# Two expert stores moved from the SyncE queue into the GpSimd ring, behind the last weight load

## The chip, the cores and the metric

The kernel runs on one core of a Trainium2 chip. The metric is the time on the device in microseconds, the median over several executions. Three executions of the kernel before gave 185.68, 185.75 and 185.85 us, so the median is 185.75 us. The execution that was profiled spans 183.8 us from its first to its last instruction; all positions in time below are microseconds from the start of that span.

## The reference

Eight experts, each with its own tokens and its own two weight matrices, computed independently:

```python
n_experts, capacity, hidden, expert_hidden = 8, 256, 512, 2048
# x [8,256,512]  w1 [8,512,2048]  w2 [8,2048,512]  b1 [8,2048]  b2 [8,512], all float32
h = np.matmul(x, w1) + b1[:, np.newaxis, :]
h = np.maximum(h, 0)
return (np.matmul(h, w2) + b2[:, np.newaxis, :]).astype(np.float32)
```

Each weight matrix of each expert is 4 MB in float32 in the device's memory (HBM), and is used once. Together with x the kernel has to read 71.4 MB, and it has to write 4.2 MB of output, 512 KB for each expert.

## The kernel before, in words

Every load of weights is a DMA issued from GpSimd that casts float32 to float16 on its way into the on-chip memory (SBUF), so a matrix of 4 MB arrives as 2 MB. Such a matrix is one DMA, with two exceptions: `w2` of expert 6 comes in two halves of 1 MB (`load_w2`, L78), and `w2` of the last expert, 7, comes in eight pieces (`load_w2_piece`, L87). A piece is named here by its place: p0 holds rows 0 to 3 of the 16 blocks of the inner dimension, p1 rows 4 to 6, p2 rows 7 to 9, p3 rows 10 and 11, all of the full width of 512 columns. Then the columns are cut at 320: p4 and p5 hold rows 12, 13 and 14, 15 of the first 320 columns, p6 and p7 the same rows of the last 192 columns.

For expert e, `first_product` (L107) multiplies x with w1 on TensorE (PE) in 16 blocks, and ScalarE (ACT) adds b1 and applies the maximum with zero. `second_product` (L150) multiplies the result with w2 and adds b2 in PSUM, and `store` (L133) copies the two halves of the result out of PSUM, one on VectorE (DVE, L137) and one on ACT (L138), into a tile of `out_pool`, which has three buffers. The main loop (L240) runs eleven steps: in step s it does the first product of expert s and the second product of expert s - 3. So the second products of experts 5, 6 and 7 fall in steps 8, 9 and 10, in which there is no first product left, and the work on PE in these steps follows directly on the arrival of w2.

The order of the DMAs on GpSimd is written out by hand. The list `ring` (L220 to L238) holds entries of a step, a function and its arguments; at the start of step s all entries at the head of the list that are due are issued (L241 to L243). GpSimd issues them in this order, and each waits for the DMA that came eight places earlier on GpSimd to land, since the DMAs of GpSimd share eight semaphores.

How an expert's output is stored depends on its number:

- Experts 0 to 4 (`e <= RING`, L143): the store is put aside in `pending` and issued from GpSimd by `flush` (L129), at its place in the ring. The store of expert 3 lies ahead of p0, that of expert 4 between p0 and p1.
- Experts 5 and 6 (L148): the store is issued from the SyncE queue (SP) as soon as the copies are done.
- Expert 7: its first 320 columns are stored from SP at L148 in one DMA of 320 KB. Its last 192 columns are stored in two DMAs of 96 KB, from SP (L141) and from ACT (L142).

The profile calls the queue of GpSimd q0, that of SP q1 and that of ACT q10. All three are served by the same 16 DMA engines of the core.

Of the kernel before, what the change touches and what calls it, by code (L numbers as in the profile page):

```python
# [11 lines left out]
def kernel(  # L12
# [17 lines left out]
    nJ = M // P  # L30
    HL = 320
    LAG = 3
    RING = 4
    PARTS = {}
    nXF32 = 2

# [96 lines left out]
    def store(e, po, c0, c1, split):  # L133
        w = c1 - c0
        pool = out_pool if w == H else singles
        out_sb = pool.tile([P, nTB, w], fp32, tag=f"out{c0}_{w}", name=f"out{w}")
        nc.vector.tensor_copy(out=out_sb[:, 0, :], in_=po[0])  # L137
        nc.scalar.copy(out=out_sb[:, 1, :], in_=po[1])  # L138
        dst = out[e].rearrange("(p tb) h -> p tb h", tb=nTB)[:, :, c0:c1]
        if split and c1 == H:  # L140
            nc.sync.dma_start(out=dst[:, 0, :], in_=out_sb[:, 0, :])  # L141
            nc.scalar.dma_start(out=dst[:, 1, :], in_=out_sb[:, 1, :])  # L142
        elif e <= RING:  # L143
            pending[e] = (dst, out_sb)
        else:
            step = P // PARTS.get(e, 1)
            for lo in range(0, P, step):
                nc.sync.dma_start(out=dst[lo : lo + step], in_=out_sb[lo : lo + step])  # L148

    def second_product(e):  # L150
# [18 lines left out]
        for lo, hi, p0, p1, t in w2_sb[e]:  # L169
            mine = [b for b in blocks if p0 <= b[0] and b[1] <= p1]  # L170
            for tb in range(nTB):
                for j in range(lo, hi):
                    for c0, c1, _, _ in mine:
                        ordered(nc.tensor.matmul(  # L174
                            out=acc[c0, tb],
                            lhsT=hT[e][:, j, tb * P : (tb + 1) * P],
                            rhs=t[:, j - lo, c0 - p0 : c1 - p0],
                            start=False,
                            stop=(j == nJ - 1),
                        ))  # L180
            if hi == nJ:
                for c0, c1, _, _ in mine:
                    store(e, [acc[c0, tb] for tb in range(nTB)], c0, c1, e == E - 1)
# [36 lines left out]
    ring = []  # L220
# [9 lines left out]
    e = E - LAG - 1  # L230
    for piece in (
        (0, 4, 0, H), (4, 7, 0, H), (7, 10, 0, H), (10, 12, 0, H),
        (12, 14, 0, HL), (14, 16, 0, HL), (12, 14, HL, H), (14, 16, HL, H),
    ):
        ring.append((0, load_w2_piece, (E - 1,) + piece))
        if e <= RING:
            ring.append((e + LAG + 1, flush, (e,)))
            e += 1  # L238

    for s in range(E + LAG):  # L240
        while ring and ring[0][0] <= s:  # L241
# [37 lines left out]
```

## Time and profile before

| what | value |
|---|---|
| median of three executions | 185.75 us |
| span of the profiled execution | 183.8 us |
| HBM read / written | 71.39 MB / 4.19 MB |
| PE busy | 137.3 us (75%) |
| ACT busy | 62.7 us (34%) |
| DVE busy | 13.3 us (7%) |
| GpSimd busy | 21.0 us (11%) |
| packets on q0, share of 16 DMA engines' span | 95.3% (37.76 MB) |
| packets on q1 | 3.1% (2.00 MB) |
| packets on q10 | 1.1% (0.69 MB) |
| store of expert 5: issued, landed after | 160.9 us, 8.2 us |
| store of expert 6: issued, landed after | 168.5 us, 7.1 us |
| last load, p7: issued, landed after | 169.34 us, 10.0 us |
| last stores of expert 7: issued, landed after | 180.16 and 180.23 us, 2.7 and 2.4 us |

The profile counts a load by the bytes that arrive, so a load in float16 counts half of what is read from HBM, and a store counts in full. The share of the DMA engines in a stretch can pass 1.00[...]. An idle time is put down to what ended it. "Landed" is the moment when the semaphore of a DMA had its full count, counted from the start of the issuing instruction. [...]

### The profile page before, as it was taken

The numbers are of one execution on the slowest core, as the hardware profiler recorded it, in microseconds if no ns is written. First come the engines' busy times: TensorE is split into PE (matmuls) and PEld (weight loads), VectorE is DVE, ScalarE is ACT, GpSimd is POOL, SyncE is SP. The second block draws the span as 40 slices with busy tenths as digits, with TensorE's granted clock in tenths as the row PEclk, the third lists the DMA queues.
The fourth block names the chain that finished last, engine by engine and source line by source line (L and its number), as shares of the span: only waits on it lengthen the run. The fifth ranks groups of instructions, "written<-read, shape, count | busy, mean of one in ns | idle before, by whom it ended". The sixth has DMA issues, their size and how long they took to land.

```text
span 183.8 us, 2205 instructions
## 1 busy us (share of the span) xinstructions
PE 137.3 (75%) x946; PEld 98.2 (53%) x946; DVE 13.3 (7%) x22; ACT 62.7 (34%) x138; POOL 21.0 (11%) x44
## 2 busy tenths in 40 slices
PE   0555969487471999569991999529999996998581
PEld 0544959387461846556491846427469543344360
DVE  0320101001000101010100100001010010101000
ACT  0022869578260422715081513605129310101001
POOL 7100030301200011011011002000022004113000
PEclk9999999999876699979999699965999999999998
DMA  5999999899999999999999999899999999999993
GB/s 185 283 207 198 228 228 210 184 233 230 228 203 196 228 228 217 194 216 228 228 210 200 217 228 228 191 266 225 207 200 270 240 209 260 214 275 310 261 151 116
DMA packets 7017, 40.58 MB, mean 221 GB/s; under 512 B 1216, under 2 KB 2256, under 8 KB 4960
## 3 DMA queue, kind: packets, MB, share of 16 engines
q0 software_dynamic: 5584, 37.76, 95.3%
q1 hardware_dynamic: 976, 2.00, 3.1%
q10 hardware_dynamic: 448, 0.69, 1.1%
q8 instruction: 7, 0.11, 0.2%
q14 instruction: 2, 0.02, 0.0%
HBM read 71.39 MB, written 4.19 MB: 411 GB/s over the span
## 4 chain that ended last, share of the span: by engine, by line
DMA 70%; PE 14%; issue 9%; another core or an unknown queue 3%; POOL 2%; ACT 0%; POOLq 0%
DMA x<-in_x_dram 24%; DMA w2sb<-in_w_dram 21%; DMA w1sb<-in_w_dram 13%; DMA w<-in_w_dram 12%; PE ph L112 6%; PE acc L174 6%; PE psx L99 1%; POOL w2sb L84 1%; POOL w1sb L74 1%; POOL out_dram L131 0%; PE acc L162 0%; POOL b_sb L190 0%; POOL ident masks.py:199 0%; POOL ident masks.py:197 0%
## 5 line engine op out<-in xcount | busy, mean ns | idle before, releaser
L112 PE MATMUL ph<-xT,w1sb 128*128 128x256 f16 x512 | 68.2, 299 | 11.6 <-DMA w1sb<-in_w_dram 11.6
L119 ACT ACTIVATE hT<-ph,b1T 128x256 f16<-128x256 f32 x128 | 57.0, 474 | 44.2 <-PE ph L112 44.2
L112 PEld LDWEIGHTS <-w1sb 128*128 128x128 f16 x512 | 61.5, 149 | 17.7 <-DMA w1sb<-in_w_dram 12.6
L174 PE MATMUL acc<-w2sb,hT 128*128 128x512 f16 x224 | 49.5, 379 | 1.6 <-DMA w2sb<-in_w_dram 1.6
L174 PEld LDWEIGHTS <-hT 128*128 128x128 f16 x288 | 27.2, 98 | 35.0 <-issue 9.0
L138 ACT COPY out<-acc 128x512 f32<-128x512 f32 (+2 forms) x9 | 4.9, 543 | 62.0 <-PE acc L174 62.0
L99 PE MATMUL psx<-ident,x 128*128 128x128 f16 x64 | 6.7, 266 | 18.8 <-DMA x<-in_x_dram 18.1
L99 PEld LDWEIGHTS <-x 128*128 128x128 f16 x64 | 5.2, 127 | 19.8 <-DMA x<-in_x_dram 19.0
L105 DVE COPY xT<-psx 128x1024 f16<-128x1024 f16 x8 | 5.5, 692 | 82.2 <-PE psx L99 82.2
L74 POOL DMA_DIRECT2D w1sb<-in_w_dram x8 | 4.4, 554 | 59.6 <-PE ph L112 58.8
L137 DVE COPY out<-acc 128x512 f32<-128x512 f32 (+2 forms) x9 | 5.7, 632 | 75.5 <-PE acc L174 75.5
L174 PE MATMUL acc<-w,hT 128*128 128x320 f16 (+1 forms) x64 | 7.7, 272 | 3.8 <-DMA w<-in_w_dram 3.7
L84 POOL DMA_DIRECT2D w2sb<-in_w_dram x8 | 4.3, 537 | 49.4 <-PE acc L174 49.4
L205 PE MATMUL pb<-ident,b_rows 16*64 16x16 f32 x64 | 3.7, 265 | 6.8 <-DMA b_rows<-in_b_dram 6.8
L205 PEld LDWEIGHTS pb<-ident,b_rows 16*64 16x64 f32 x64 | 3.6, 198 | 6.8 <-issue 6.8
L90 POOL DMA_DIRECT2D w<-in_w_dram x8 | 5.0, 623 | 13.0 <-DMA w2sb<-in_w_dram 8.8
L119 ACT ACT_TABLE_LOAD x1 | 1.3, 1283 | 11.2 <-DVE b1T L213 11.2
L131 POOL DMA_DIRECT2D out_dram<-out x5 | 2.7, 540 | 19.5 <-ACT out L138 13.1
L162 PE MATMUL acc<-b_sb,ones 1*128 1x512 f16 (+2 forms) x18 | 4.8, 355 | 0.0
L68 POOL DMA_DIRECT2D x<-in_x_dram x6 | 3.3, 546 | 7.2 <-DMA w2sb<-in_w_dram 5.1
L162 PEld LDWEIGHTS <-ones 1*128 1x128 f16 x18 | 1.1, 92 | 2.2 <-issue 2.1
L200 DVE CAST x<-x 128x1024 f16<-128x1024 f32 x2 | 1.4, 694 | 4.5 <-DMA x<-in_x_dram 4.5
(9 smaller groups left out, 2.6 us busy)
## 6 DMA issues: line engine op xcount, KB each, us to landing
w1sb<-in_w_dram POOLq DMA_DIRECT2D x8, 2048.0 KB, 33.7
w2sb<-in_w_dram POOLq DMA_DIRECT2D x6, 2048.0 KB, 45.7
out_dram<-out POOLq DMA_DIRECT2D x5, 512.0 KB, 40.1
w2sb<-in_w_dram POOLq DMA_DIRECT2D x2, 1024.0 KB, 24.6
x<-in_x_dram POOLq DMA_DIRECT2D x6, 256.0 KB, 39.0
out_dram<-out SPq DMA_DIRECT2D x2, 512.0 KB, 7.6
w<-in_w_dram POOLq DMA_DIRECT2D x2, 384.0 KB, 20.8
x<-in_x_dram SPq DMA_DIRECT2D x1, 512.0 KB, 4.7
```

What stands on the lines that cost most here:

```text
L74: ordered(nc.gpsimd.dma_start(out=w1_sb[e], in_=w1[e].rearrange("(p kc) m -> p kc m", kc=nKC)))
L84: ordered(nc.gpsimd.dma_start(out=t[:, lo : lo + step, :], in_=src[:, lo : lo + step, :]))
L90: ordered(nc.gpsimd.dma_start(out=t, in_=src[:, lo:hi, c0:c1]))
L99: ordered(nc.tensor.transpose(out=pt[:, kc, tb * P : (tb + 1) * P], in_=x16[e][:, tb, :].rearrange("p (q kc) -> p q kc", kc=nKC)[:, :, kc] ...
L105: nc.vector.tensor_copy(out=xT[e], in_=pt)
L112: ordered(nc.tensor.matmul(out=ph, lhsT=w1_sb[e][:, kc, :].rearrange("p (q j) -> p q j", j=nJ)[:, :, j], rhs=xT[e][:, kc, :], start=(kc == 0),
L119: nc.scalar.activation(out=hT[e][:, j, :], in_=ph, func=mybir.ActivationFunctionType.Relu, bias=b1T[:, j, e : e + 1], scale=1.0,)
L137: nc.vector.tensor_copy(out=out_sb[:, 0, :], in_=po[0])
L138: nc.scalar.copy(out=out_sb[:, 1, :], in_=po[1])
L162: ordered(nc.tensor.matmul(out=t, lhsT=ones1, rhs=b2_sb[0:1, e * H + c0 : e * H + c1], start=True, stop=False,))
L174: ordered(nc.tensor.matmul(out=acc[c0, tb], lhsT=hT[e][:, j, tb * P : (tb + 1) * P], rhs=t[:, j - lo, c0 - p0 : c1 - p0], start=False, sto ...
L205: ordered(nc.tensor.matmul(out=pb[s * 64 : (s + 1) * 64, j, :, :], lhsT=b1_rows.rearrange("r (q j) -> r q j", j=nJ)[:, :, j], rhs=ident[0 ...
```

## The change

The stores of experts 5 and 6 are no longer issued from SP. They are put aside like those of experts 0 to 4, and are issued from GpSimd as the last two entries of the ring, after p7. The entry for expert 5 is due in step 9 and that for expert 6 in step 10. The aim is that these two stores no longer share the DMA engines with the loads that the last second product waits for. Nothing else is edited: the other stores, the loads and their order, and all of the arithmetic stay.

```diff
     LAG = 3
-    RING = 4
+    LATE = (5, 6)
+    RING = (0, 1, 2, 3, 4) + LATE
...
-        elif e <= RING:
+        elif e in RING:
             pending[e] = (dst, out_sb)
...
         ring.append((0, load_w2_piece, (E - 1,) + piece))
-        if e <= RING:
+        if e in RING and e not in LATE:
             ring.append((e + LAG + 1, flush, (e,)))
             e += 1
+    for e in LATE:
+        ring.append((e + LAG + 1, flush, (e,)))
```

In the order of instructions that results, SP keeps its load of x and its two stores of expert 7 and loses two stores; GpSimd gains two stores behind p7. PE, DVE and ACT keep their instructions and their order. The new store of expert 5 waits on GpSimd for the store of expert 4 (eight places earlier) and for its copies, the new store of expert 6 for p1 and its copies.

## The prediction

> **What bounds the kernel now.** I read the page first (busy shares, slices, queues), then the DMA engines in short stretches of the end, then each late DMA's time to landing, then the last instructions in order of time. From the page:
>
> ```profile
> DMA  5999999899999999999999999899999999999993
> ...
> q0 software_dynamic: 5584, 37.76, 95.3%
> q1 hardware_dynamic: 976, 2.00, 3.1%
> ```
>
> The DMA engines are full from the first slice to the last, while PE is busy 75% of the span. So the kernel ends when its bytes have moved, plus whatever must follow the last load. The stretches of the end show that tail (the last two columns are the DMA engines' share and GB/s by arriving bytes):
>
> ```profile
> 143.60:151.00 7.40, 7.40 (x34) 3.05 (x32) 0.69 (x1) 0.45 (x2) 0.00 (x0) 1.00 0.99 213
> 162.00:168.40 6.40, 6.33 (x31) 2.84 (x30) 0.69 (x1) 0.52 (x1) 1.42 (x2) 1.00 1.00 303
> 170.40:172.00 1.60, 0.61 (x6) 0.39 (x5) 0.00 (x0) 0.00 (x0) 0.00 (x0) 1.00 1.07 213
> 172.00:175.00 3.00, 1.47 (x12) 1.09 (x12) 0.00 (x0) 0.00 (x0) 0.00 (x0) 1.00 1.07 289
> 175.00:177.40 2.40, 1.95 (x18) 1.60 (x18) 0.00 (x0) 0.00 (x0) 0.00 (x0) 1.00 1.33 194
> 177.40:179.00 1.60, 1.60 (x14) 1.13 (x13) 0.23 (x1) 0.00 (x0) 0.00 (x0) 1.00 0.72 87
> 179.00:180.60 1.60, 0.82 (x9) 0.45 (x6) 0.62 (x2) 0.74 (x2) 0.00 (x0) 1.00 0.00 0
> 180.60:182.60 2.00, 0.00 (x0) 0.00 (x0) 0.00 (x0) 0.00 (x0) 0.00 (x0) 0.99 0.81 266
> ```
>
> Loads alone arrive at 213 GB/s (first and third row). Where the figure is nearer 300, stores share the engines. Then the engines go part idle (177.4 to 179.0) and wholly idle (179.0 to 180.6): nothing is left to move until expert 7's result is ready. That hole is the room for this change. Times to landing, in order: the stores of experts 5 and 6 from SP (issued at 160.94 and 168.5), the store of expert 4 from GpSimd (152.04), p0 (138.42), p1 (152.57), p2 (153.43), p7 (169.34):
>
> ```profile
> out_dram<-out SPq DMA_DIRECT2D x1, 512.0 KB, 8.2
> ...
> out_dram<-out SPq DMA_DIRECT2D x1, 512.0 KB, 7.1
> ```
>
> ```profile
> out_dram<-out POOLq DMA_DIRECT2D x1, 512.0 KB, 18.3
> ```
>
> ```profile
> w<-in_w_dram POOLq DMA_DIRECT2D x1, 512.0 KB, 30.6
> w<-in_w_dram POOLq DMA_DIRECT2D x1, 384.0 KB, 19.6
> w<-in_w_dram POOLq DMA_DIRECT2D x1, 384.0 KB, 22.0
> w<-in_w_dram POOLq DMA_DIRECT2D x1, 96.0 KB, 10.0
> ```
>
> So p0 lands at 169.0, expert 4's store at 170.3, p1 at 172.2, p2 at 175.4, p7 at 179.34. The chain that ended last closes on p7:
>
> ```profile
> 175.45 3.88 PE acc L174 x32
> 179.34 0.02 issue
> 179.35 0.50 PE acc L174 x4
> 179.85 0.02 issue
> 179.88 0.32 ACT out L138
> ```
>
> PE's last four matmuls start 0.01 us after p7 lands. Copies end at 180.2, the stores are issued at 180.16 and 180.23 and land at 182.86 (180.16 + 2.7); the span ends 0.95 us later.
>
> [...]213 GB/s becomes 289 to 303 when a store is in flight, and p2 arrives late (below). [...]an SP store of 512 KB took 7 to 8 us among loads, where expert 4's, in order behind p0 in q0, landed 1.3 us after p0. [...]
>
> **The change part by part.**
>
> *Removed: two SP stores among the loads.* What they cost the loads follows from landing steps. A step of 384 KB at 213 GB/s is 393,216 B / 213 = 1.85 us. From expert 4's store to p1 the step is 1.9 us, undisturbed. From p1 to p2, the same size, it is 3.3 us with expert 6's store in flight: 1.4 us for that store. For expert 5's: the second half of expert 6's w2 lands at 164.2 (issued at 137.4, 26.8 us), the store of expert 3 at 165.9 (137.89 + 28.0), p0 at 169.0. The halves of w2 are 5.0 us apart, 4.9 at the pure rate: 0.1 lost. The store of expert 3 took 1.7 against 1.3 for that of expert 4: 0.4 lost. p0 took 3.1 against 524,288 B / 213 = 2.5: 0.6 lost. That is 1.1 to 1.2. Both together 2.6 us. Bounds: all of q1's 2.00 MB cost 3.1% of 183.8 us, 5.7 us, or 351 GB/s, which makes 3.0 us for 1.05 MB. From 162.0 to 168.4, 1.94 MB arrived; with two stores in it (1.05 MB) the loads are 0.89 MB or 4.2 us at 213, and 2.2 us remain for 1.05 MB. I take 2.6, ends 2.2 and 3.0. Nothing before 160.9 moves.
>
> *Moved: the loads and PE.* p0 is then due at 167.8, p1 at 170.9, p2 at 172.8, p7 at 176.7. Can PE follow? It finishes expert 6 and the bias of expert 7 at 168.3 as before. The 64 matmuls of the pieces took 1.91 + 1.47 + 4.39 = 7.8 us, so from 168.3 alone the end would be 176.1: earlier than p7, so the loads still set it. From p2 at 172.8 the last 36 need at most 4.4 us: 177.2. From p7: 176.7 + 0.5 = 177.2. Both agree: PE ends 2.6 us earlier, the copies at 177.6, the last stores are issued about then.
>
> *Added: two GpSimd issues.* A store's issue from GpSimd took 0.54 us, two 1.1 us. The first waits for expert 4's store (due at 169.1), the second for p1 (170.9), and the copies of experts 5 and 6 are done by 161 and 168.5. They are issued by 171.5, with p2 to p7 still ahead in q0, and nothing is queued behind them on GpSimd. Cost nothing, hidden under those loads. No buffer waits either: nothing is written to `out_pool` after expert 6.
>
> *Added: 1.05 MB at the end of q0.* In order behind p7, at the 1.3 us step of expert 4's store: 178.0 and 179.3. Ends: 1.1 us each, from 140.4 to 142.8, where a store raised q0's rate to 329 GB/s with no other queue at work (0.79 MB in 2.4 us; if all 0.52 MB of the store fell in it, the loads took 1.3 us and the store 1.1); and 1.5 us each at q1's price. So 178.9 to 179.7[...]. The part-idle engines of 177.4 to 179.0 help here: with work behind p7 they have something to take.
>
> *Who waits for that.* Only the end of the program, and the last stores of expert 7 (0.52 MB), which share the engines with it. Before, their bytes moved from about 180.75 to 182.4. Alone they would move from 178.1. Until expert 6's bytes are out, some 0.4 us ahead of landing, at 178.9, [...]0.8 us at half rate, 0.4 us lost. Landing: 182.86 - 2.6 + 0.4 = 180.7. This is later than the 179.3 that I take, so expert 7's stores still end the kernel. Gain 2.2 us: 185.75 - 2.2 = 183.5 us.
>
> A check by the bytes: all data have to move either way, and the only thing the change can win is the hole, 1.6 us wholly idle, about 0.1 at its edge and 1.6 times (1 - 0.72) = 0.4 part idle, or 2.1 us. The sums agree.
>
> **The rivals.** *Part of the gain given back at the end (184.5 us).* The late stores move at q1's price and wholly ahead of expert 7's: 176.3 + 3.0 = 179.3 for the bytes, 1.65 us for expert 7's, 0.45 to land: 181.4, a gain of 1.5; if the removal also brings only 2.2, about 1.2. For it: pure stores at 180.6 to 182.6 ran no faster than some 340 GB/s. Against: these have short rows, the moved ones 4 KB.
>
> *The loads come no earlier (185.6 us).* If the small pieces p4 to p7 were limited by their own row sizes (194 and 87 GB/s) and not by what went before, the gain would be swallowed there. Against: the pieces land one behind the other, and p7 is 3.9 us behind p2 with all stores gone by then, so a shift of p2 passes through.
>
> *The late stores become the end (186.3 us, slower).* [...]For it: no store in this trace is last in q0. Against: expert 4's store landed 1.3 us behind p0[...].
>
> **How the numbers follow.** Forecast 72%, given back in part 14%, no earlier 5%, late stores 9%. Predicted 183.5. Low end: 3.0 us removed and 0.2 lost in turns, 182.95, so 182.9. High end: the first rival with 0.3 us of reserve, 184.8. Outside lie the last two rivals, 14%, and a few per cent below. Faster by over 0.2% (0.37 us): 0.72 + 0.14 + 0.01 = 0.87; within 0.04; slower 0.09.
>
> **What would show it.** Right: SP shows no 512 KB store; the step from p1 to p2 falls from 3.3 to about 1.9 us; p7 lands near 176.7; PE's last matmul ends near 177.2; the wholly idle stretch of the DMA engines after the last load is gone; expert 6's store lands 2 to 3 us behind p7 and ahead of expert 7's. Wrong: p7 lands where it did; PE runs without a gap from 168.3 and ends later than p7 + 0.5; expert 7's stores take much over 3.1 us; or the last landing is a store from GpSimd.

## The result and the profile after

The changed kernel took 183.69 us (median of 5, from 183.47 to 183.89), the kernel before 185.68 us beside it (median of 5, from 185.57 to 185.85). The ratio is 0.9889, with a 95% interval from 0.9876 to 0.9903: 2.0 us faster, where 2.2 us were forecast. A second measurement, together with the later experiments, gave 183.74 against 185.78 us.

From the page of the changed kernel, the DMA lines and the queues:

```profile
DMA  5989998999899999999999999999899989999994
...
q0 software_dynamic: 5872, 38.81, 97.8%
q1 hardware_dynamic: 688, 0.95, 1.6%
```

1.05 MB went over from q1 to q0. In slices as long as these (4.5 us) the engines look as full as before. The span is 181.7 us in place of 183.8 for the same bytes, so the mean rate over the span, bytes read from HBM and written to it, rose from 411 to 416 GB/s. The end in the same stretches as in the prediction (the first figure after the length is the busy time of PE, the last two columns are the DMA engines' share and GB/s; a share above 1.00, here up to 1.31, says that packets on one engine overlapped):

```profile
170.40:172.00 1.60, 1.04 (x10) 0.85 (x10) 0.00 (x0) 0.00 (x0) 0.75 (x2) 1.00 1.07 207
172.00:175.00 3.00, 2.58 (x24) 2.01 (x23) 0.00 (x0) 0.00 (x0) 0.08 (x1) 1.00 1.31 202
175.00:177.40 2.40, 2.28 (x18) 1.41 (x16) 0.72 (x2) 0.50 (x2) 0.00 (x0) 1.00 1.14 364
177.40:179.00 1.60, 0.00 (x0) 0.00 (x0) 0.12 (x1) 0.25 (x1) 0.00 (x0) 1.00 0.75 288
179.00:180.60 1.60, 0.00 (x0) 0.00 (x0) 0.00 (x0) 0.00 (x0) 0.00 (x0) 1.00 0.55 189
```

From 172 to 175, loads alone now arrive at 202 GB/s where loads and a store together made 289. From 175.0 to 177.4 it is 364 instead of 194, since the late stores follow the last loads. The stretch from 179.0 to 180.6, in which nothing moved, now moves 189 GB/s. PE is busy for 2.58 us of the stretch from 172 to 175, before for 1.47: it waits less for its pieces.

The landings: p1 and p2 (issued at 152.45 and 153.46), p7 (168.11), then the late stores of experts 5 and 6 (170.12 and 171.53), then expert 7's last two (177.59 from SP, 177.68 from ACT), the first of each pair of lines being the earlier:

```profile
w<-in_w_dram POOLq DMA_DIRECT2D x1, 384.0 KB, 18.5
w<-in_w_dram POOLq DMA_DIRECT2D x1, 384.0 KB, 19.3
w<-in_w_dram POOLq DMA_DIRECT2D x1, 96.0 KB, 8.7
...
out_dram<-out POOLq DMA_DIRECT2D x1, 512.0 KB, 7.9
out_dram<-out POOLq DMA_DIRECT2D x1, 512.0 KB, 7.8
...
out_dram<-out SPq DMA_DIRECT2D x1, 96.0 KB, 3.1
out_dram<-out ACTq DMA_DIRECT2D x1, 96.0 KB, 2.7
```

So p1 lands at 170.95, p2 at 172.8, p7 at 176.8, expert 5's store at 178.0, expert 6's at 179.3 and expert 7's last at 180.7. The chain that ended last closes on p7 as before, 2.5 us earlier:

```profile
172.85 3.94 PE acc L175 x32
176.79 0.01 issue
176.80 0.51 PE acc L175 x4
```

PE and the loads gained 2.5 us (the last four matmuls start at 176.80, before at 179.35). Expert 7's last store takes 3.1 us instead of 2.7, and this 0.4 is what the late stores gave back here.

Two profiles need not reach the end of the kernel in step, even where nothing that was changed has run yet. The second product of expert 5 starts when its w2 lands, and no run of this document changes a DMA ahead of that w2 in the queue; it starts at 153.18 us before and at 153.22 after, and between 152.94 and 153.71 in the experiments:

```profile
153.18 5.12 PE L174 MATMUL acc<-w2sb,hT 128*128 128x512 f16 x23 [1.57 <-DMA w2sb<-in_w_dram]
153.22 5.12 PE L175 MATMUL acc<-w2sb,hT 128*128 128x512 f16 x23 [1.73 <-DMA w2sb<-in_w_dram]
```

Counted from this start, p7 comes 2.6 us earlier than before and the end of the span 2.1 us earlier.

### The profile page after: what moved, and what is told of

It reads as the page before. It is cut to its first block, busy times and chain, and to the rows that moved or that the text cites. A ratio compares the mean times of both kernels' runs of the same rounds, so it can differ in the third digit from the quotient of the medians.

```text
span 181.7 us, 2204 instructions
## 1 busy us (share of the span) xinstructions
PE 137.0 (75%) x946; PEld 97.9 (54%) x946; DVE 13.3 (7%) x22; ACT 62.7 (35%) x138; POOL 22.2 (12%) x46
## 4 chain that ended last, share of the span: by engine, by line
DMA 70%; PE 14%; issue 9%; another core or an unknown queue 3%; POOL 2%; ACT 0%; POOLq 0%
DMA x<-in_x_dram 24%; DMA w2sb<-in_w_dram 22%; DMA w1sb<-in_w_dram 13%; DMA w<-in_w_dram 11%; PE ph L113 6%; PE acc L175 6%; PE psx L100 1%; POOL w2sb L85 1%; POOL w1sb L75 1%; POOL out_dram L132 0%; PE acc L163 0%; POOL b_sb L191 0%; POOL ident masks.py:199 0%; POOL ident masks.py:197 0%
## 5 line engine op out<-in xcount | busy, mean ns | idle before, releaser
L132 POOL DMA_DIRECT2D out_dram<-out x7 | 3.8, 544 | 21.6 <-ACT out L139 13.1
```

## The experiments

All experiments start from the changed kernel. Each was timed together with the kernel before on the same chip, which took 185.73, 185.78 or 185.59 us there; the ratios are to that. The theory, from the prediction: a store ahead of p7 delays p7 by its own time on the engines, in whichever queue; the stores are best placed directly behind p7, where the engines had nothing to do; and what is won is bounded by that idle time. Rivals: that the SP queue was the trouble and not the place, that one store of the two makes the gain, that it only matters not to be ahead of p7, and that the late stores cost nothing.

From the profiles, in us, with the last two columns counted from the start of expert 5's second product:

| kernel | that start | p7 lands | p7 from there | end of the span from there |
|---|---|---|---|---|
| before | 153.18 | 179.31 | 26.1 | 30.6 |
| changed | 153.22 | 176.76 | 23.5 | 28.5 |
| changed, repeated | 153.27 | 176.79 | 23.5 | 28.5 |
| both stores left out | 153.41 | 176.93 | 23.5 | 28.0 |
| expert 5's late, expert 6's left out | 153.71 | 177.25 | 23.5 | 28.0 |
| only expert 6's late | 152.94 | 178.03 | 25.1 | 29.5 |
| only expert 5's late | 153.03 | 177.87 | 24.8 | 29.4 |
| expert 5's ahead of three loads | 153.11 | 177.89 | 24.8 | 29.3 |
| both behind expert 7's stores | 153.50 | 177.03 | 23.5 | 31.0 |
| three late, spare matmuls | 153.18 | 175.51 | 22.3 | 28.5 |
| two late, spare matmuls | 153.30 | 176.82 | 23.5 | 28.5 |

### Both stores left out

```diff
-    for e in LATE:
-        ring.append((e + LAG + 1, flush, (e,)))
...
-    assert not ring and not pending
+    assert not ring
```

> The stores of experts 5 and 6 are left out altogether; everything else is as in the changed kernel. This measures the removal alone, and by the difference to the changed kernel what the late stores cost at the end. My theory (two stores less ahead of p7 bring 2.6 us, the late stores give 0.4 to 0.5 back by sharing the engines with expert 7's stores): p7 lands at 176.8, PE ends at 177.3, expert 7's last store takes 2.7 us again and not 3.1, 183.2 us. Rival (the late stores are free, and the 0.4 us are lost for another reason, such as a slower issue on SP): 183.7 us, and expert 7's stores still take 3.1 us.

183.07 us, ratio 0.9851 [0.9836, 0.9867]. p7 landed at 176.9 (issued at 168.28), and the stores of expert 7, the first 320 columns and the last 192 from SP and from ACT, took the old times:

```profile
w<-in_w_dram POOLq DMA_DIRECT2D x1, 96.0 KB, 8.7
out_dram<-out SPq DMA_DIRECT2D x1, 320.0 KB, 2.8
out_dram<-out SPq DMA_DIRECT2D x1, 96.0 KB, 2.7
out_dram<-out ACTq DMA_DIRECT2D x1, 96.0 KB, 2.4
```

The removal alone is worth 185.73 - 183.07 = 2.7 us (2.6 forecast), and putting the stores behind p7 costs 0.6 to 0.7 us of that (183.69 and 183.74 against 183.07). By the spans in the table it is 2.6 and 0.5 us. The rival of free late stores falls: without them, the 3.1 us are 2.7 again.

### Only one store left out

```diff
-    LATE = (5, 6)
-    RING = (0, 1, 2, 3, 4) + LATE
+    LATE = (5,)
+    RING = (0, 1, 2, 3, 4) + LATE + (6,)
...
-        if e in RING and e not in LATE:
+        if e == 4:
...
-    assert not ring and not pending
+    assert not ring
```

> Expert 6's store is left out, expert 5's is late as in the changed kernel: half of the late bytes. My theory: 0.52 MB behind p7 are out by 177.7, before expert 7's bytes start, so they cost nothing and the time is that with both left out, 183.2 us. Rival (each late store costs its half): halfway to the changed kernel, 183.4 to 183.5 us.

183.01 us, ratio 0.9848 [0.9835, 0.9862], and expert 7's last store took 2.7 us. With 0.52 MB behind p7 nothing is lost that can be measured; the second 0.52 MB costs all of the 0.6 to 0.7 us. The packets by queue from 178.2 to 180.6 us, in which expert 7's bytes move, bear on this. In the changed kernel 0.07 MB of the late stores is still to move when expert 7's bytes begin, at 178.2. The first line has the engines' share in 40 slices, each of 0.06 us:

```profile
DMA  6988979999999988998999999753321210000000
...
q1 hardware_dynamic: 412, 0.42, 49.4%
q10 hardware_dynamic: 144, 0.10, 12.3%
q0 software_dynamic: 24, 0.07, 7.2%
```

With one store late nothing is left in q0 when they begin, at 178.7:

```profile
DMA  0000000059999999999999999999999996300000
...
q1 hardware_dynamic: 416, 0.43, 51.9%
q10 hardware_dynamic: 144, 0.10, 12.8%
```

0.07 MB at the rate of these stretches, some 350 GB/s, are only 0.2 us. But in the changed kernel the share falls off slowly, from 179.7 to 180.2, where with one store it breaks off within some 0.1 us. That fits engines that still had a late store's packets and so finished expert 7's later than the others; the view does not part the engines, so this much of the cause is argued and not shown.

### Only expert 6's store late, then only expert 5's

```diff
-    LATE = (5, 6)
+    LATE = (6,)
```

```diff
-    LATE = (5, 6)
+    LATE = (5,)
```

The store that is not late goes out on SP as in the kernel before.

> Only expert 6's store is late, expert 5's stays on SP. My theory (each store costs the loads its own share, 1.4 us for expert 6's, and 0.52 MB at the end find room in the idle stretch): p7 lands at 178.0, 184.3 us. Rival (the gain is won by one store, the second adds nothing, since PE sets the end by then): 183.7 us. Rival (the gain hangs on both being off the SP queue): within 0.4 us of 185.7.

> Only expert 5's store is late, expert 6's stays on SP. My theory: 1.2 us less ahead of p7, so p7 at 178.1 and 184.5 us. Rival (expert 5's store lies beside work of PE that is bound by PE until 168.3, so its removal brings nothing): p7 at 179.3, 185.7 us.

184.24 us, ratio 0.9919 [0.9904, 0.9933], and 184.29 us, ratio 0.9921 [0.9905, 0.9936]: 1.5 and 1.4 us faster. p7 landed at 178.03 (169.23 + 8.79) and at 177.87 (167.92 + 9.95), first with expert 6's store late, then with expert 5's. Each line of p7 is followed by the start to count from:

```profile
w<-in_w_dram POOLq DMA_DIRECT2D x1, 96.0 KB, 8.8
...
152.94 5.34 PE L175 MATMUL acc<-w2sb,hT 128*128 128x512 f16 x24 [1.78 <-DMA w2sb<-in_w_dram]
```

```profile
w<-in_w_dram POOLq DMA_DIRECT2D x1, 96.0 KB, 9.9
...
153.03 5.34 PE L175 MATMUL acc<-w2sb,hT 128*128 128x512 f16 x24 [1.36 <-DMA w2sb<-in_w_dram]
```

Each store has its own share, so the rivals of one store, of both together, and of an expert 5 hidden beside PE fall. Counted from that start, p7 came 1.0 us earlier with expert 6's store late and 1.3 with expert 5's, where the prediction had 1.4 and 1.2; with both it is 2.6, so the two delays do not simply add. In neither run is expert 7's last store delayed (2.7 us). By the times the two gains add up to 2.9 us, 0.9 more than the two stores bring together; by the spans in the table they are 1.1 and 1.2 us, 0.2 more than both. What two late stores cost at the end, 0.5 to 0.7 us, is part of either difference. The times and the profiles do not agree on the rest.

### The same queue, but ahead of three loads

Expert 5's store in the GpSimd ring ahead of p5, expert 6's last:

```diff
-    LATE = (5, 6)
-    RING = (0, 1, 2, 3, 4) + LATE
+    LATE = (6,)
+    RING = (0, 1, 2, 3, 4, 5) + LATE
...
-        if e in RING and e not in LATE:
-            ring.append((e + LAG + 1, flush, (e,)))
-            e += 1
+        if piece[0] == 0:
+            ring.append((8, flush, (4,)))
+        if piece == (12, 14, 0, HL):
+            ring.append((9, flush, (5,)))
```

> Both stores are in the GpSimd queue, but expert 5's lies ahead of p5, so three loads follow it; expert 6's is last as in the changed kernel. It tells the queue from the place. My theory (the place counts: a store ahead of p5 costs p7 its 1.2 to 1.3 us in either queue): p7 lands at 178.0, 184.4 us, as with expert 5's store on SP. Rival (the SP queue is what costs[...]; in the GpSimd queue a store costs the loads little): p7 near 177, 183.8 us.

184.18 us, ratio 0.9910 [0.9897, 0.9924], the same as with expert 5's store on SP (184.24). p7 was issued at 169.57:

```profile
w<-in_w_dram POOLq DMA_DIRECT2D x1, 96.0 KB, 8.3
```

It landed at 177.9, against 178.0 with that store on SP. So the place ahead of p7 costs in the GpSimd queue as well, and not only on SP. In the table p7 comes 0.3 us earlier than with that store on SP (24.8 against 25.1), and the times differ by 0.06 us with intervals that overlap: the place makes the larger part, and whether SP adds a little, one profile of each does not settle.

### Late, but behind expert 7's stores

```diff
-    for e in LATE:
-        ring.append((e + LAG + 1, flush, (e,)))
...
+    for e in LATE:
+        dst, src = pending.pop(e)
+        nc.sync.dma_start(out=dst, in_=src)
     assert not ring and not pending
```

> Both stores are late but on SP, behind expert 7's stores, not behind p7 in the GpSimd queue. My theory (the gain is made of two halves: the loads come earlier, and the late bytes fill the stretch in which the engines were idle): the loads and PE gain 2.5 us as in the changed kernel, but 1.05 MB then move after expert 7's stores, 2.5 to 3.0 us, and the time is that of the kernel before, 185.4 to 185.9 us. Rival (it is enough that the stores don't lie ahead of p7, wherever they go): 183.7 us.

185.70 us, ratio 1.0002 [0.9992, 1.0011]. The time is as expected, but not for the reason. Where the order on SP is not held by `ordered`, it is worked out when the program is built, and the issues show that the two stores were placed ahead of expert 7's, since they depend on nothing later:

```profile
162.46 7.88 SPq L251 DMA_DIRECT2D out_dram<-out  x2
179.47 0.61 SPq L149 DMA_DIRECT2D out_dram<-out  x1
```

They ran beside the loads, and p7 landed at 179.3 as in the kernel before. This run therefore repeats the kernel before, with the stores issued 1.5 us later (162.46 and 170.01 for 160.94 and 168.49), and says nothing about the end. In the next one the order on SP is held to that written:

```diff
-            nc.sync.dma_start(out=dst[:, 0, :], in_=out_sb[:, 0, :])
+            ordered(nc.sync.dma_start(out=dst[:, 0, :], in_=out_sb[:, 0, :]))
...
-                nc.sync.dma_start(out=dst[lo : lo + step], in_=out_sb[lo : lo + step])
+                ordered(nc.sync.dma_start(out=dst[lo : lo + step], in_=out_sb[lo : lo + step]))
...
+    for e in LATE:
+        dst, src = pending.pop(e)
+        ordered(nc.sync.dma_start(out=dst, in_=src))
```

> The two stores on SP behind expert 7's stores, this time with the order on SP held to that written (in the run before, they were moved ahead of expert 7's stores and ran beside the loads from 162.5). My theory (the loads come earlier, but the late bytes miss the stretch in which the engines are idle): p7 lands at 176.8, expert 7's last store at 180.3, then 1.05 MB in about 2.5 us; the span ends near 183.5 and the time is 185.2 to 185.8 us, no gain. Rival (only the place ahead of p7 counts): 183.7 us.

186.22 us, ratio 1.0035 [1.0023, 1.0046]: slower than before, and 0.4 us above the range that I expected. p7 landed at 177.0. SP's issues and the engines at the end:

```profile
177.87 0.59 SPq L142 DMA_DIRECT2D out_dram<-out  x1
178.50 0.99 SPq L251 DMA_DIRECT2D out_dram<-out  x2
```

```profile
176.60:178.00 1.40, 0.94 (x9) 0.57 (x7) 0.73 (x2) 0.74 (x2) 0.00 (x0) 1.00 0.01 1
178.00:180.00 2.00, 0.00 (x0) 0.00 (x0) 0.00 (x0) 0.00 (x0) 0.00 (x0) 1.00 0.77 266
180.00:182.00 2.00, 0.00 (x0) 0.00 (x0) 0.00 (x0) 0.00 (x0) 0.00 (x0) 0.64 1.03 408
182.00:184.50 2.50, 0.00 (x0) 0.00 (x0) 0.00 (x0) 0.00 (x0) 0.00 (x0) 0.50 0.24 93
```

The loads came over 2 us earlier here as well, and it did not help: the engines stood idle from 176.6 to 178.0 and then had 1.05 MB to move at some 400 GB/s behind expert 7's bytes. Expert 7's last store landed at 180.6 and the second of the late stores 2.9 us behind it, where I had put 2.5. So it is not enough that the stores are out of the way of p7. They have to lie where the engines are idle.

### A third late store, and a PE that can follow

```diff
-    LATE = (5, 6)
-    RING = (0, 1, 2, 3, 4) + LATE
+    LATE = (4, 5, 6)
+    RING = (0, 1, 2, 3) + LATE
```

> The store of expert 4 goes behind p7 as well, so three stores are late. My theory (only an idle engine can be won, and after the change some 0.4 us of it is left): p7 lands at 175.5, PE ends at 176.2 and is then bound by PE, but 1.57 MB follow, and expert 7's stores land 0 to 0.4 us earlier than in the changed kernel: 183.3 to 183.7 us. Rival (each store moved brings 1.0 us more): 182.7 us. Rival (three stores are too many, the late ones end the kernel): 184.2 us or more.

183.66 us, ratio 0.9885 [0.9872, 0.9899], no different from the changed kernel beside it. But its profile does not tell bytes from PE. p7 landed at 175.7, and PE ended only at 177.3, with no wait left, because the 32 matmuls of expert 5's second product, after 2.00 us of idle PE, took 8.75 us and not 7.07, at a granted clock of 0.64 from 153.4 to 157.5 us:

```profile
153.40 8.75 PE L175 MATMUL acc<-w2sb,hT 128*128 128x512 f16 x32 [2.00 <-DMA w2sb<-in_w_dram]
162.08 0.60 PE L163 MATMUL acc<-b_sb,ones 1*128 1x512 f16 x2
162.61 7.08 PE L175 MATMUL acc<-w2sb,hT 128*128 128x512 f16 x32
169.63 0.61 PE L163 MATMUL acc<-b_sb,ones 1*128 1x320 f16 x4
170.16 7.16 PE L175 MATMUL acc<-w,hT 128*128 128x320 f16 x64
```

The same kernel with six spare matmuls in that wait, and the changed kernel with them as its partner:

```diff
+                spare = 6 if e == 5 and tb == 0 else 0
+                for n in range(spare + 1):
-                ordered(nc.tensor.matmul(
+                    ordered(nc.tensor.matmul(
...
-                    stop=False,
+                        stop=n < spare,
```

> The stores of experts 4, 5 and 6 are late, and six spare matmuls of b2 (overwritten by the real one, so the result is the same) fill PE's wait for expert 5's w2, after which the profile of three late stores showed a granted clock of 0.72 and 1.7 us more of PE work. Theory A (with three late stores PE sets the end): PE ends near 176.2 instead of 177.3, and the time falls to 183.0 to 183.4 us. Theory B (the bytes set the end): PE ends near 176.2, but expert 7's stores take 3.7 to 4.2 us instead of 3.1, and the time stays at 183.5 to 183.8 us.

> The changed kernel with the same six spare matmuls. Both theories: PE ends at 177.3 because p7 lands at 176.8, so 183.5 to 183.8 us. Faster by 0.3 us or more would say that the lower clock cost the changed kernel something in the timed runs.

With three late stores 183.41 us, ratio 0.9878 [0.9863, 0.9893]; with two 183.53 us, ratio 0.9886 [0.9873, 0.9900]. In the first, expert 5's matmuls took 7.07 us and PE ended at 176.05. Expert 7's stores, the first 320 columns from 175.64 and the rest from 176.31 and 176.43, then took:

```profile
out_dram<-out SPq DMA_DIRECT2D x1, 320.0 KB, 4.5
out_dram<-out SPq DMA_DIRECT2D x1, 96.0 KB, 4.3
out_dram<-out ACTq DMA_DIRECT2D x1, 96.0 KB, 4.0
```

They landed at 180.6, where they land at 180.7 in the changed kernel: PE won 1.2 to 1.3 us, and the stores gave back 1.2 (the last one took 4.3 us, 0.1 more than theory B had). That is theory B; the time, 183.41, lies 0.1 us below its range and just above the range of theory A. The bytes set the end now. Whether three late stores are a little better than two (183.24 to 183.44 against 183.34 to 183.66) the times don't settle, as the intervals overlap; in the profiles both spans end 28.5 us after the start of expert 5's second product, so no gain is seen there. It is the lowest time of a full kernel in this study.

With two late stores the clock fell in spite of the spare matmuls (to a mean of 0.62 from 153.4 to 157.5 us; expert 5's took 8.75 us), so that run does not show the changed kernel without the fall. Its first profile and its repeat do: expert 5's matmuls took 7.07 us in the one and 8.75 in the other, and both spans end 28.5 us after they start. The fall costs the changed kernel nothing that can be measured.

### Fewer short rows

```diff
-        (12, 14, 0, HL), (14, 16, 0, HL), (12, 14, HL, H), (14, 16, HL, H),
+        (12, 14, 0, H), (14, 16, 0, HL), (14, 16, HL, H),
```

The six spare matmuls are in this kernel too, so its partner is the changed kernel with them, 183.53 us.

> The changed kernel with the spare matmuls, and with p4 and p6 in one load of the full width (rows 12 and 13, 512 columns) ahead of p5 and p7, so the loads have fewer short rows. If the short rows cost the loads what their steps show (p3 to p7 took 2.8 us for 512 KB where the pure rate makes 2.5), p7 lands 0.1 to 0.3 us earlier and the time is 183.3 to 183.6 us. If they cost nothing that counts: 183.7 us.

183.69 us, ratio 0.9896 [0.9883, 0.9910]. The last load landed at 177.0 (166.02 + 11.0), 23.5 us after the start of expert 5's second product (153.54), as in the partner. Joining the short rows of two loads brought nothing that counts here.

### The changed kernel again

> The changed kernel again, beside the others on the same chip: 183.7 us.

183.74 us, ratio 0.9888 [0.9874, 0.9901]. In its profile expert 5's second product took 8.75 us, as with three late stores, and PE worked without a gap from there to 177.34, where p7 landed at 176.8. In the first profile PE waited for p7 and ended at 177.31. The two limits lie within some 0.1 us of each other.

## Why the prediction was right

**The bound and the hole.** Right. The engines set the end, and what could be won was the stretch without work behind p7. The two kernels whose late bytes miss it or overfill it show the bound from both sides: behind expert 7's stores they cost more than was won (1.0035), and a third late store bought 1.2 us on PE and gave it back.

**What the two stores cost the loads, 2.6 us.** Right in the sum: p7 landed at 176.8 where 176.7 was forecast, and leaving both out is worth 2.7 us by the times and 2.6 by the profiles. The split, 1.2 and 1.4 for experts 5 and 6, is not confirmed: taken out of the way alone, expert 5's store brought p7 forward by 1.3 us and expert 6's by 1.0. The step from expert 4's store to p1 was rightly taken as undisturbed, though expert 6's store had been issued before it, at 168.49: from 168.6 to 171.8 q1 moved a single packet.

**PE follows.** Right, with p7 the last wait and PE's end at 177.3 for 177.2. It was closer than the prediction allowed: the reserve of 1.1 us between PE's own limit (176.1) and p7's supposed that all matmuls run at full clock, and in other profiles of these kernels 1.7 us were lost, more than the reserve. In the repeat of the changed kernel PE had no gap, which the prediction had named as a sign of being wrong. That PE's own limit then came within 0.1 us of p7's, and cost nothing, was luck.

**The GpSimd issues cost nothing.** Right: they start at 170.12 and 171.53, with p2 to p7 still to land.

**The steps of the late stores, 1.3 us each.** Right: 178.0 and 179.3, both as forecast. The landing step of expert 4's store was a better price than the bounds: the steps here were 1.2 and 1.3 us for 512 KB. The rival in which the late stores become the end (186.3 us) was the author's estimate and was not shown: expert 6's store landed at 179.3, 1.4 us ahead of expert 7's last. Alone in q0 the late stores reached 410 GB/s (176.9 to 177.2), above the 345 of expert 7's stores in the kernel before (181 to 182); that the rows of 4 KB make this difference was not shown.

**Sharing with expert 7's stores, 0.4 us.** Right in kind, small in size: 0.4 us in the landing of expert 7's last store, 0.5 by the spans in the table, 0.6 to 0.7 by the medians without the two stores. The last and the 0.1 more for the removal make the 2.0 us that were measured of the 2.2 forecast. The times at which the queues meet were right too: expert 7's bytes begin at 178.2 (178.1 forecast), and the last packets of q0 end at 179.0 (178.9). But the working, 0.8 us at half rate, was not what happened. The half rate was the author's estimate; from 178.2 to 179.0 q0 moved only 0.07 MB, and q1 0.22. Nor was the sharing the same in both stretches of the kernel before in which a store from SP ran beside the loads: with expert 5's (164.5 to 168.6) q1's packets took 33.1% of the engines' time and q0's 69.9%, with expert 6's (171.9 to 174.6) it was 48.1% and 56.9%. From 177.6 to 178.2 q0's packets took 48.4% of it, so the late stores no longer filled all of them before expert 7's bytes came. The size of this term was met in part by luck.

## What to carry to other kernels

Where the DMA engines set the time, as here, a store that is not needed by anyone belongs behind the last load that someone waits for, and right behind it: there it fills the time in which the last results are computed, while behind the last results it cost more here than was won (186.22 us against 185.59 before). How much can be won is read from the idle stretch of the DMA engines between the last load and the last store (2.1 us here, of which 2.0 were won); one late store was free here, the second cost 0.5 to 0.7 us, and a third bought next to nothing. The difference between the landing times of two neighbours in one queue gave the price of a transfer better here (1.3 us forecast, 1.2 and 1.3 measured) than the share of its queue (1.5), as long as nothing else moves between them (from p1 to p2 it was 1.9 us in the changed kernel, and 3.3 before with expert 6's store in flight). And where two profiles are compared by a few tenths of a us, count from a point that the change cannot reach.

## What the runs showed of the hardware that was not expected

In some executions the granted clock of PE fell to 0.50 around the start of expert 5's second product, in the repeat of the changed kernel from 153.8 to 157.2 us, and 32 matmuls took 8.60 to 8.75 us in place of 7.07: 3.4 us at half the clock make the 1.7 us lost there. In the profiles without spare matmuls it fell where PE had been idle for 2.00 to 2.79 us before (five of them), and not where it had been idle for 1.25 to 1.78 us (six, with that of the kernel before).

How long PE was idle does not explain it alone. From 151.0 to 153.4 us PE was busy for 1.36 us in the changed kernel with spare matmuls, and the clock fell (to a mean of 0.62 from 153.4 to 157.5); in the changed kernel without them PE was busy for 0.67 us there, and the clock stayed at 1.00. With three late stores and the spare matmuls PE was busy for 2.08 us, and the clock stayed at 1.00 too. What decides it, these profiles don't tell.

Earlier in the kernel before, the clock was at 0.50 in five stretches, from 49.45, 56.27, 80.17, 100.64 and 121.12 us, for 3.41 us or, the second and the last, 6.83 us. PE waited for its loads before or into each of them, for 3.29 to 5.57 us. These five starts lie whole multiples of 3.413 us apart, within 0.01 us.

A store from SP waited long beside a full GpSimd queue: in the kernel before its first packet moved 3.6 us after its issue for expert 5 (160.94 to 164.5) and 3.4 us for expert 6 (168.49 to 171.9), where expert 7's, with the engines idle, took 1.3 us (179.49 to 180.75). What it waits for, these profiles don't tell.
